# Head 1's input projections as seven block products instead of eight, with the sums of inputs formed beside the latent projections

## The chip, the cores and the metric

One Trainium2 chip, one core of it. The metric is the device time of one execution in microseconds (us), lower is better. The kernel computes one inference step of a one-layer encoder for 544 tokens (512 of a new stream, 32 of a running one).

The engines are named as in the profile: PE is the matrix engine (TensorE), DVE the VectorE, ACT the ScalarE, POOL the GpSimd; SP only issues transfers. Each engine takes its own row of instructions in order and waits at an instruction until what it needs is there.

## The reference, cut to what matters

```python
def token_mixer(x, s0, lat_past, kr_past, blk, lb, w_in, ...):
    proj = x @ w_in                       # x: 544 tokens x 2048 features
    hq, hf, hi, hg, cq, ckv, kr = jnp.split(proj, SPLITS, axis=-1)
    f = lb + (1.0 - lb) * jax.nn.sigmoid(hf)
    o_h, s_new = hgrn2_recurrence(heads(hq), heads(1.0 - f), heads(jnp.log(f)), heads(hi), s0, blk)
    o_h = rms_norm(o_h, ...) * jax.nn.silu(hg)
    ...                                   # latent attention from cq, ckv, kr -> o_a
    out = jnp.concatenate([o_h, o_a], axis=-1) @ w_out

def encoder(x, ...):
    h = layer_norm(x, ...)
    mix = token_mixer(h, ...)
    h = layer_norm(ALPHA * h + mix, ...)
    ff = conv_ffn(h, ...)                 # two projections up to 5632 features, one down
    h = layer_norm(ALPHA * h + ff, ...)
```

There are 8 recurrent heads and 8 attention heads. The change touches the projections `x @ w_in` of recurrent head 1 (its q, f, i and g columns, 128 each).

## The kernel before, in words

All products are in split form for accuracy: each 32-bit operand is written as a high part (`wh`, `aH`, made by a copy on ACT) and a low part (`wl`, `aL`, made by a subtraction on DVE), and three matmuls are summed (high x high, high x low, low x high). A weight piece is loaded by SP into one of three `raw` buffers (`load_raw`, L123), and ACT and DVE split it (`split_w`, L128).

The order of the stages is that of the code: layer norm and the projection cq (until about 78 us); ckv (`ckv_proj`, 77.9 to 104.8) and kr (`kr_proj`); the two projections q and f of head 0 (`head_qf(0)`, four weight pieces of 48 matmuls, from 112.7); four pairs of attention heads (`proj_pair`, `attend`); i and g of head 0 (`head_ig(0)`, beside the last `attend`); head 1 (296 to about 372); heads 2 to 7 (until 696); then the output projection (until about 850) and the convolutional FFN, which the change does not touch.

`weave` (L191) mixes two sequences in program order: after so many steps of the filling one, one step of the chain, such as `ckv_norm` (L487) with its two rows `lx` of the normalised latent, or `kr_rope`. A few instructions of `ckv_norm` are PE's: sums over the features (L441) after the first 24 matmuls of `head_qf(0)`, and a spread over partitions (L450, L451) after 72.

Heads 2 to 7 are projected in a divided form (`divided`, L828): the 2 x 2 blocks of the input (features x tokens, 272 tokens each) and of the weights are combined as in Winograd's form of Strassen's product, so that seven block products of 24 matmuls do instead of eight. The seven are named "11", "s1", "s2", "s4", "s3", "12", "22"; "s1" to "s4" use sums of input blocks, which are formed once (`sums_of_inputs`, L724): with t0 and t1 the two token halves of a feature row, and t0b, t1b those of the row 1024 features on, the sums are t0 - t1, t1b - t1 and two that follow from them. Each is split into a high and a low part. s1, s2 and s4 stay in SBUF; s3 goes through DRAM and is then laid over the second halves of `aH` and `aL` (`place_s3`). The weights' sums are formed per group: DVE adds blocks (L780) and POOL issues accumulating transfers (L782, L795). In the same place (`low`, L791) POOL issues up to two further accumulating transfers, the `forms`, by which block sums of `w_out` are prepared in DRAM for the output stage, which is divided too.

Heads 0 and 1 are done plainly (`N_PLAIN = 4` groups of two projections: 192 matmuls each). While head 1 is done, the sums of inputs are formed from the rows `h0` of the normalised input, reloaded from DRAM; beside it run `levels(0)`, `levels(1)` and `finish(0)`, the recurrences of heads 0 and 1. In `levels`, Kp and Qp are formed on DVE, then PE and DVE alternate through seven levels.

From head 2 on the order on PE, DVE and ACT is that of the code (`tc.manual_schedule`), by slots: each product has two, and `beside_from` says in which slots a step of `levels` or `finish` is put.

The memory for the recurrences (`gp`) opens when that of attention (`mp`) closes. Its tiles wait for the last users of what lay there, such as the store of `attend`'s last difference (L669, L670).

Of the kernel before, what the change touches and what calls it, by code (L numbers as in the profile page):

```python
# [15 lines left out]
P = 128  # L16
# [39 lines left out]
N_PLAIN = 4  # L56
# [3 lines left out]
def tile_encoder_step(ctx, tc, xp, xs, w_in, w_in4, w_kr, w_q_b, w_kv_b, w_out, w_out4, w_up, w_gate, w_down, w_down2,  # L60
# [16 lines left out]
    d3_dr = [dram.tile([P, 2, NI], F32, name=f"d3d{k}", tag=f"d3d{k}") for k in range(HK // 2)]  # L77
    sm_dr = [dram.tile([P, 3, 4, NI], F32, name=f"sm{i}", tag=f"sm{i}") for i in range(2)]
# [321 lines left out]
    with tc.tile_pool(name="mp", bufs=1) as mp, tc.tile_pool(name="psa", bufs=4, space=PSUM) as psa:  # L400
        cos = mp.tile([P, T], F32, name="cos")
        sin = mp.tile([P, T], F32, name="sin")
# [7 lines left out]
        ropes = [[mp.tile([P, TP], R, name=f"qr{g}{j}", tag=f"qr{g}{j}") for j in range(2)] for g in range(2)]  # L410

# [58 lines left out]
        def cq_norm():  # L470
            rb, rb2 = yield from rms_rows(sq_sum(cqx), 512)
            for k in range(4):
# [4 lines left out]
                h, l = split_act(x, bufs=4, pool=mp, th="qaH", tl="qaL")  # L477
# [9 lines left out]
        def ckv_norm():  # L487
            rb, rb2 = yield from rms_rows(c["kvs"], 256)
            for k in range(2):
                x = c["kv"][k]  # L490
                lx = mp.tile([P, NK], F32, name="lx", tag="lx", bufs=1)
# [7 lines left out]
                h, l = split_act(lx, bufs=2, pool=mp, th="latH", tl="latL", n=NK)  # L499
# [37 lines left out]
        def proj_pair(pr):  # L537
# [46 lines left out]
            vt = mp.tile([P, 6, 2, P], F32, name="vt", tag="vt")  # L584
# [13 lines left out]
        def softmax(sc, nq, keys):  # L598
            mx = mp.tile([P, 1], F32, name="mx", tag="mx", bufs=4)
            rs = mp.tile([P, 1], F32, name="rsum", tag="rsum", bufs=4)  # L600
            p = mp.tile([P, 512], F32, name="p", tag="p", bufs=3)
# [7 lines left out]
        def attend(pr):  # L609
            qn, qr, kn, vt = pairs[pr]  # L610
            o = mp.tile([P, 2, T], F32, name="o", tag="o")
# [67 lines left out]
        weave([ckv_proj(), kr_proj()], [cq_norm()], 0.5, tick)  # L679
        weave([head_qf(0)], [ckv_norm(), kr_rope()], 0.5, tick)  # L680
        while len(forms) > 24:
            form_next()
        run(proj_pair(0))
        weave([proj_pair(1)], [attend(0)], 2.0)
        weave([proj_pair(2)], [attend(1)], 2.0)
        weave([proj_pair(3)], [attend(2)], 2.0)
        weave([head_ig(0)], [attend(3)], 2.0)
# [12 lines left out]
    s3_dr = [dram.tile([P, 2, NI], F32, name=f"s3d{k}", tag=f"s3d{k}") for k in range(HK)]  # L700


    with tc.tile_pool(name="gp", bufs=1) as gp, tc.tile_pool(name="psg", bufs=1, space=PSUM) as psg:
# [9 lines left out]
        sums = {n: [gp.tile([P, 2, 4, NI], R, name=f"{n}{i}", tag=f"{n}{i}") for i in range(2)] for n in ("s1", "s2", "s4")}  # L713

        def part(n, k, i):
            return sums[n][k // 4][:, i, k % 4]

        def load_sums():
            for k in range(HK):
                for dst, kg, j in (("s1", k, 1), ("s2", k, 0), ("s4", HK + k, 0)):  # L720
                    dma(part(dst, k, 1).bitcast(F32), h0_dr[kg][:, H_[j]])
                dma(part("s1", k, 0).bitcast(F32), h0_dr[HK + k][:, H_[1]])

        def sums_of_inputs():  # L724

            load_sums()
            for k in range(HK):
# [304 lines left out]
        def early_form():  # L1032
            ticks[0] += 1
            if ticks[0] in (6, 9, 12, 15):
                form_next()
# [1621 lines left out]
```

## Time and profile before

| What | Before |
|---|---|
| Device time, median of 3 runs | 2337.82 us (2337.44 to 2337.97) |
| Profiled execution, its own time | 2336.92 us |
| Its span, first to last instruction | 2335.1 us |
| Mean granted PE clock | 0.994 |
| PE busy | 2295.9 us (98%) |
| DVE busy | 1713.1 us (73%) |
| ACT busy | 1095.4 us (47%) |
| POOL busy | 271.3 us (12%) |
| Moved by DMA | 474.57 MB, mean 203 GB/s |

The span is what the profile's times count from; the time of an execution holds a little more at both ends. A row of the profile names a line of the kernel, an engine, an operation, what it writes and what it reads; in brackets stands how long the engine was idle before it and what ended that. "Granted clock" is the share of full speed that the throttle gave PE. A DMA's time to landing runs from its issue to the arrival of its last byte.

### The profile page before, as it was taken

To read this page: it belongs to the slowest core of one execution; us is meant where nothing else is said; L and a number is where in the kernel's file an instruction comes from. 1 tells how busy PE (TensorE), PEld (TensorE's weight loads), DVE (VectorE), ACT (ScalarE), POOL (GpSimd) and SP (SyncE) were. 2 spreads that over 40 slices of the span, in tenths; PEclk is the share of its full clock that TensorE was granted. 3 is DMA by queue.
4 is the path that set the end of the run, shared out by engine and by line. 5 is a ranking of instruction groups with operands and counts; after the bars stand their busy time and mean duration, and the time that the engine had idled before them with its cause. 6 is when DMAs were issued, how large, how long until landed. Compare 5 with 4: busy or idle time off the path is not lost.

```text
span 2335.1 us, 44650 instructions
## 1 busy us (share of the span) xinstructions
PE 2295.9 (98%) x18258; PEld 2279.5 (98%) x18258; DVE 1713.1 (73%) x2393; ACT 1095.4 (47%) x1686; POOL 271.3 (12%) x335
## 2 busy tenths in 40 slices
PE   7999999999999999999999999999999999999997
PEld 7999999999999999999999999999999999999997
DVE  7455567777776878987777777777777677777776
ACT  6345434343444537655555555555555433333324
POOL 1011001111101111010000000100001111111102
PEclk9999999999999999999999999999999999999998
DMA  7432277676766756777667676776777999889832
GB/s 262 144 108 95 73 220 181 175 169 194 166 186 221 251 160 219 211 198 217 194 180 230 169 205 204 177 230 179 188 221 187 367 325 309 264 273 309 285 106 79
DMA packets 175773, 474.57 MB, mean 203 GB/s; under 512 B 16080, under 2 KB 80336, under 8 KB 168144
## 3 DMA queue, kind: packets, MB, share of 16 engines
q1 hardware_dynamic: 140368, 320.76, 39.7%
q0 software_dynamic: 35200, 150.94, 28.1%
q8 instruction: 144, 2.36, 0.4%
q14 instruction: 61, 0.50, 0.1%
HBM read 394.36 MB, written 91.34 MB: 208 GB/s over the span
## 4 chain that ended last, share of the span: by engine, by line
PE 92%; DVE 2%; ACT 2%; DMA 1%; issue 1%; POOL 0%; SPq 0%; ACTq 0%; DVEq 0%; POOLq 0%
PE main L1319 22%; PE acc L1319 17%; PE main L1350 11%; PE main L851 10%; PE main L146 10%; PE acc L1350 7%; PE acc L146 3%; PE s L916 2%; PE sb L1804 1%; PE main L1804 1%; PE main L591 1%; PE at L652 1%; PE at L621 1%; DMA xr<-wf1s 1%; PE main L578 0%
## 5 line engine op out<-in xcount | busy, mean ns | idle before, releaser
L1261 DVE TENSOR_TENSOR wl<-raw,wh 128x1024 fp32r<-128x1024 f32 x371 | 456.2, 1230 | 193.2 <-ACT wh L1260 192.9
L1260 ACT ACTIVATE wh<-raw 128x1024 fp32r<-128x1024 f32 x371 | 392.1, 1059 | 408.9 <-PE main L1319 99.3
L1319 PE MATMUL main<-op,wh 128*128 128x272 f32 x1408 | 265.4, 288 | 0.0
L1319 PE MATMUL acc<-ops,wh 128*128 128x272 f32 x1344 | 254.1, 288 | 0.0
L1319 PE MATMUL main<-ops,wh 128*128 128x272 f32 x1344 | 254.1, 288 | 0.0
L1319 PEld LDWEIGHTS main<-op,wh 128*128 128x128 f32 x1408 | 221.2, 188 | 0.0
L1319 PEld LDWEIGHTS acc<-ops,wh 128*128 128x128 f32 x1344 | 211.2, 188 | 0.0
L1319 PEld LDWEIGHTS main<-ops,wh 128*128 128x128 f32 x1344 | 211.1, 188 | 0.0
L1319 PE MATMUL main<-op,wl 128*128 128x272 f32 x704 | 203.1, 288 | 0.3 <-DVE wl L1261 0.3
L1319 PE MATMUL main<-ops,wl 128*128 128x272 f32 x672 | 193.9, 289 | 0.0
L1319 PE MATMUL acc<-ops,wl 128*128 128x272 f32 x672 | 193.9, 288 | 0.0
L1319 PE MATMUL acc<-op,wh 128*128 128x272 f32 x832 | 157.5, 288 | 1.0 <-ACT ea L1645 1.0
L1260 ACT ACTIVATE wh<-rawl 128x1024 fp32r<-128x1024 f32 x93 | 98.8, 1063 | 117.3 <-PE acc L1319 45.8
L146 PE MATMUL main<-aH,wh 128*128 128x272 f32 (+2 forms) x608 | 149.3, 297 | 0.3 <-ACT wh L316 0.2
L146 PE MATMUL main<-aH,wl 128*128 128x272 f32 (+2 forms) x608 | 147.8, 293 | 1.8 <-DVE wl L317 1.8
L146 PE MATMUL main<-aL,wh 128*128 128x272 f32 (+2 forms) x608 | 146.4, 292 | 1.0 <-DVE aL L305 1.0
L1261 DVE TENSOR_TENSOR wl<-rawl,wh 128x1024 fp32r<-128x1024 f32 x93 | 113.8, 1224 | 27.0 <-ACT wh L1260 26.9
L1319 PEld LDWEIGHTS main<-op,wl 128*128 128x128 f32 x704 | 132.4, 188 | 0.5 <-DVE wl L1261 0.5
L1319 PEld LDWEIGHTS acc<-op,wh 128*128 128x128 f32 x832 | 130.5, 188 | 1.2 <-ACT ea L1645 1.2
L793 DVE TENSOR_TENSOR wl<-raw,wh 128x1024 fp32r<-128x1024 f32 x84 | 103.1, 1227 | 35.9 <-ACT wh L788 35.0
L1319 PEld LDWEIGHTS main<-ops,wl 128*128 128x128 f32 x672 | 126.4, 188 | 0.0
L1319 PEld LDWEIGHTS acc<-ops,wl 128*128 128x128 f32 x672 | 126.4, 188 | 0.0
(513 smaller groups left out, 6090.8 us busy)
## 6 DMA issues: line engine op xcount, KB each, us to landing
raw<-in_w_in SPq DMA_DIRECT2D x76, 512.0 KB, 5.1
raw<-in_w_up SPq DMA_DIRECT2D x71, 512.0 KB, 5.2
raw<-in_w_gate SPq DMA_DIRECT2D x71, 512.0 KB, 4.8
raw<-in_w_down SPq DMA_DIRECT2D x67, 512.0 KB, 9.2
opd<-ohl SPq DMA_DIRECT2D x20, 1088.0 KB, 5.5
ops<-opd POOLq DMA_DIRECT2D x20, 1088.0 KB, 12.0
raw<-in_w_up POOLq DMA_DIRECT2D x35, 512.0 KB, 5.2
opd<-ohl SPq DMA_DIRECT2D x20, 816.0 KB, 6.4
```

Source lines behind the costliest of these rows:

```text
L146: PE.matmul(ps, ww[:, wcols[0]:wcols[1]], aa[:, hs[j]], start=first and i == 0, stop=last and i == 2, skip_group_check=True)
L591: PE.matmul(ps[:, j * 512:j * 512 + 256], l[k][:, a:b], r4(w[:, k:k + 1, :])[:, 0, :, 128:256], start=k == 0 and i == 0, stop=k == 1 and i ...
L621: PE.matmul(sc[:, :nk], qn[j][:, q0:q0 + P], kn[j][:, :nk], start=True, stop=False)
L652: PE.matmul(po[:, :P], vt[:, k, j, :], t[:, k * P:(k + 1) * P], start=k == 0, stop=k == b)
L793: V.tensor_tensor(out=wl, in0=self.t(self.key), in1=wh.bitcast(F32), op=ALU.subtract)
L851: PE.matmul(out, ww[:, k * P:(k + 1) * P], aa, start=name in ("11", "s1", "12") and k == 0 and q == 0, stop=k == HK - 1 and q == 2, skip_g ...
L916: PE.matmul(ps[:, j * 64:(j + 1) * 64], Kp[:, a:b], Qv[:, j * bt:(j + 1) * bt, 1, :], start=True, stop=True)
L1260: A.activation(wh, src, AF.Copy)
L1261: V.tensor_tensor(out=wl, in0=src, in1=wh.bitcast(F32), op=ALU.subtract)
L1319: PE.matmul(ps, ww[:, k * P:(k + 1) * P], aa, start=self.first and k == 0 and i == 0, stop=k == n - 1 and i == 2, skip_group_check=True)
L1350: PE.matmul(banks[:, 512 * u:512 * u + NI], ww[:, (u * n + k) * P:(u * n + k + 1) * P], aa, start=self.first and k == 0 and i == 0, stop=k ...
L1804: PE.matmul(self.bank, ww[:, k * P:(k + 1) * P], aa, start=self.first and k == 0 and i == 0, stop=k == HK - 1 and i == 2, skip_group_check ...
```

## The change

`N_PLAIN` goes from 4 to 2: head 1's two groups are divided too, so that 14 groups of seven products follow head 0. For this the sums of inputs must be there before head 1 begins.

- `sums_of_inputs` moves to the latent projections. `beside` takes a step of it after every second step of `ckv_proj`, `kr_proj` and `head_qf(0)`; each step handles a block row k of 8 in half: loads of two rows `h0`, four half-width sums on DVE; then two splits of full width and four stores to DRAM (`si_dr`). It works in tiles of attention that are not yet in use (`p`, `kn`, `o`, `vt`, `qr0`, `qr1`).
- The sums are loaded back: s1 and s2 under `head_ig(0)` and `attend(3)`, into a part of SBUF on the right side that the latent's tiles have left (`mpr`, then `smr`); s4 into `gp`; s3 is laid over `aH` and `aL` as before, from `si_dr`.
- `levels(0)` and `finish(0)` become steps in the slots of the divided part: `levels(0)` at slots 0 to 12, `finish(0)` and `levels(1)` both from slot 15.
- The four early `forms` under `head_ig(1)` are gone; the forms are issued two per group from head 1's first group on.
- In the output stage, the product "s2" of column group 2 moves ahead of "s4" of group 1, and two hooks come one item later.

```diff
-N_PLAIN = 4
+N_PLAIN = 2
...
+        def sums_of_inputs():
+            for k in range(HK):
+                tag, n, bufs = (("p", T, 3), ("kn", NK, 2))[k % 2]
+                a, b = (mp.tile([P, n], F32, name=tag, tag=tag, bufs=bufs)[:, :T] for _ in range(2))
+                dma(a, h0_dr[k])
+                dma(b, h0_dr[HK + k])
+                t0, t1, t0b, t1b = (x[:, h] for x in (a, b) for h in H_)
+                yield
+                minus(t1b, t1b, t1)
+                minus(t1, t0, t1)
+                opposite(t0, t1b, t0)
+                opposite(t0b, t0, t0b)
+                for x, names, (tag, n) in ((a, ("s2", "s3"), (("o", 2 * T), ("qr0", 2 * T))[k % 2]),
+                                           (b, ("s4", "s1"), (("vt", 12 * P), ("qr1", 2 * T))[k % 2])):
+                    hl = mp.tile([P, n], R, name=tag, tag=tag)[:, :2 * T].rearrange("p (i w c) -> p i w c", i=2, w=2)
+                    x2 = x.rearrange("p (w c) -> p w c", w=2)
+                    A.activation(hl[:, 0], x2, AF.Copy)
+                    V.tensor_tensor(out=hl[:, 1], in0=x2, in1=hl[:, 0].bitcast(F32), op=ALU.subtract)
+                    for w, name in enumerate(names):
+                        dma(si_dr[name][k // 4][:, :, k % 4], hl[:, :, w].bitcast(F32))
+                yield
...
-        weave([ckv_proj(), kr_proj()], [cq_norm()], 0.5, tick)
-        weave([head_qf(0)], [ckv_norm(), kr_rope()], 0.5, tick)
+        of_inputs = sums_of_inputs()
+        weave([beside(ckv_proj(), of_inputs, 2), beside(kr_proj(), of_inputs, 2)], [cq_norm()], 0.5, tick)
+        weave([beside(head_qf(0), of_inputs, 2)], [ckv_norm(), kr_rope()], 0.5, tick)
+        run(of_inputs)
...
+        mpr_stack.close()
...
+        for name in ("s1", "s2"):
+            load_sum(smr, name)
         weave([head_ig(0)], [attend(3)], 2.0)
...
-        of_inputs = sums_of_inputs()
-        weave([beside(head_qf(1), of_inputs, 2)], [levels(0)], 0.6)
...
-        weave([beside(head_ig(1), of_inputs, 2)], [levels(1), finish(0)], 1.2, early_form)
-        run(of_inputs)
-        place_s3()
         supply()
         for n in range(2):
             begin(n)
             complete(n)
+        load_sum(gp, "s4")
+        place_s3()
...
-            beside_from(0, finish(1), range(15))
-            for h in range(2, HEADS):
-                s0 = 28 * (h - 2) + 15
+            beside_from(0, levels(0), (0, 1, 3, 4, 6, 8, 9, 11, 12))
+            beside_from(15, finish(0), range(15))
+            for h in range(1, HEADS):
+                s0 = 28 * (h - 1) + 15
...
-            groups = [g for h in range(2, HEADS) for g in (divided_qf(h), divided_ig(h))]
+            groups = [g for h in range(1, HEADS) for g in (divided_qf(h), divided_ig(h))]
...
+        osteps += [(1, "12"), (1, "s1"), (1, "s2"), (2, "s2"), (1, "s4"), (1, "s3"), (1, "22")]
...
-                  3: [lambda: split_su("s2", 1)], 4: [lambda: split_su("s4", 0), lambda: split_su("s4", 1)],
-                  5: [lambda: split_21(range(4))], 6: [lambda: split_21(range(4, 8))],
+                  3: [lambda: split_su("s2", 1)], 4: [lambda: split_su("s4", 0)], 5: [lambda: split_su("s4", 1)],
+                  6: [lambda: split_21(range(4))], 7: [lambda: split_21(range(4, 8))],
```

The change moves instructions in the engines' rows. Before, SP's row where the weights of `head_qf(0)` are loaded: the third and fourth of its four pieces are the two loads of `raw` in one row, right behind the second and a form.

```order
L492 DMA lx<-in_latp 128x128
L125 DMA raw<-in_w_in 128x1024
L91 DMA wf3s_109<-in_w_out 16x8192
L125 DMA raw<-in_w_in 128x1024 x2
L91 DMA wf4s_113<-in_w_out 16x8192
L125 DMA raw<-in_w_q_b 128x768 x2
```

Now, SP's row behind the stores of block row 6 of the sums, up to the load of the third piece (`sis` are the sums in DRAM, `out_lat` the latent's output, `t<-t` the swapped halves of the rope).

```order
L494 DMA lx<-in_latp 128x128
L499 DMA out_lat<-lx 128x512
L500 DMA out_lat<-lx 128x32
L459 DMA t<-t 32x544
L460 DMA t<-t 32x544
L459 DMA t<-t 32x544
L460 DMA t<-t 32x544
L700 DMA sis_100<-qr_1628 256x1x272
L700 DMA sis_102<-qr_1628 256x1x272
L700 DMA sis_104<-qr_1633 256x1x272
L700 DMA sis_98<-qr_1633 256x1x272
L127 DMA raw<-in_w_in 128x1024
```

The load of the third piece stood ahead of the latent's stores and the rope's swaps; it now stands behind them and behind the stores of all eight block rows.

DVE's row before, at the splits of the third and fourth piece (the last `wl<-raw,wh 128x1024 x2`):

```order
L434 TENSOR_TENSOR t<-t 128x544
L135 TENSOR_TENSOR wl<-raw,wh 128x1024
L435 TENSOR_TENSOR t<-t 128x544
L135 TENSOR_TENSOR wl<-raw,wh 128x1024 x2
L444 TENSOR_SCALAR r_1371<-at 128x5
L523 TENSOR_TENSOR t<-t 128x544
```

And now, from block row 7 of the sums on:

```order
L186 SCALAR_TENSOR_TENSOR kn<-kn 128x272 x2
L495 SCALAR_TENSOR_TENSOR lx<-t,par,at 128x512
L497 SCALAR_TENSOR_TENSOR lx<-t,par,at 128x32
L698 TENSOR_TENSOR qr_1628<-kn,qr_1628 128x544
L698 TENSOR_TENSOR qr_1633<-kn,qr_1633 128x544
L215 TENSOR_TENSOR latL<-lx,latH 128x672
L465 TENSOR_TENSOR t<-t,sin 128x544
L467 TENSOR_TENSOR krs<-t 128x512
L467 TENSOR_TENSOR krs<-t 128x32
L532 TENSOR_TENSOR krl<-krs,krh 128x512
L137 TENSOR_TENSOR wl<-raw,wh 128x1024 x2
```

The two splits stood ahead of the first step of `ckv_norm` (L444); they now stand behind its last.

POOL's row before, where `attend(3)` ends (its difference is the second of the two `o<-o`) and the recurrences begin:

```order
L669 TENSOR_TENSOR o<-o 128x2x272 x2
L708 MEMSET attnT_3481 128x544
L708 MEMSET attnT_3482 128x544
L711 MEMSET kT 128x128
L91 DMA wf1s_99<-in_w_out 256x512
L91 DMA wf1s_101<-in_w_out 256x512
```

And now (`raw` are blocks of head 1's weights, `wf1s` the forms):

```order
L671 TENSOR_TENSOR o<-o 128x2x272
L796 DMA raw<-in_w_in 128x1024
L809 DMA raw<-in_w_in 128x1024
L93 DMA wf1s_107<-in_w_out 256x512
L93 DMA wf1s_109<-in_w_out 256x512
L671 TENSOR_TENSOR o<-o 128x2x272
L754 MEMSET attnT_3638 128x544
L754 MEMSET attnT_3639 128x544
L757 MEMSET kT 128x128
```

Four accumulating transfers now stand ahead of `attend(3)`'s difference on POOL, two for head 1's weights and two forms.

More of the change, by code (lines that the diff above doesn't have):

```diff
@@ L77, in tile_encoder_step @@
     d3_dr = [dram.tile([P, 2, NI], F32, name=f"d3d{k}", tag=f"d3d{k}") for k in range(HK // 2)]
+    si_dr = {n: [dram.tile([P, 2, 4, NI], F32, name=f"si{n}{i}", tag=f"si{n}{i}") for i in range(2)]
+             for n in ("s1", "s2", "s3", "s4")}
     sm_dr = [dram.tile([P, 3, 4, NI], F32, name=f"sm{i}", tag=f"sm{i}") for i in range(2)]
@@ L677, in tick, with beside @@
                 form_next()
-        weave([ckv_proj(), kr_proj()], [cq_norm()], 0.5, tick)
-        weave([head_qf(0)], [ckv_norm(), kr_rope()], 0.5, tick)
+        def sums_of_inputs():
[19 more added lines that the diff above has]
+                yield
+        def beside(main, side, every):
+            for n, _ in enumerate(main):
+                if n % every == every - 1:
+                    next(side, None)
+                yield
+        of_inputs = sums_of_inputs()
+        weave([beside(ckv_proj(), of_inputs, 2), beside(kr_proj(), of_inputs, 2)], [cq_norm()], 0.5, tick)
+        weave([beside(head_qf(0), of_inputs, 2)], [ckv_norm(), kr_rope()], 0.5, tick)
+        run(of_inputs)
         while len(forms) > 24:
             form_next()
+        ropes = [[t[:, j * T:j * T + TP] for j in range(2)]
+                 for t in (mp.tile([P, 2 * T], R, name=f"qr{g}", tag=f"qr{g}") for g in range(2))]
         run(proj_pair(0))
@@ L686, in tile_encoder_step, with load_sum @@
         weave([proj_pair(3)], [attend(2)], 2.0)
+        mpr_stack.close()
+        sr_stack = ExitStack()
+        smr = sr_stack.enter_context(tc.tile_pool(name="smr", bufs=1, side="right", reuse_waits="tile"))
+        sums = {}
+        def load_sum(p, name):
+            sums[name] = [p.tile([P, 8 * NI], R, name=f"{name}{i}", tag=f"{name}{i}").rearrange("p (i k c) -> p i k c", i=2, k=4)
+                          for i in range(2)]
+            for i in range(2):
+                dma(sums[name][i].bitcast(F32), si_dr[name][i])
+        for name in ("s1", "s2"):
+            load_sum(smr, name)
         weave([head_ig(0)], [attend(3)], 2.0)
@@ L1095, in tile_encoder_step @@
         out_first()
+    sr_stack.close()
     ph1.close()
```

67 lines of the change are left out of this document (15 added, 52 removed).

## The prediction

> **What bounds the kernel now.** I read the page first, then busy time by stage, then the chain of waits and the time lines of the engines around the two places that the change touches. The page says that TensorE (PE) is the bound: it is busy nearly all the time, and it is 92% of the chain that ended last.
>
> ```profile
> PE 2295.9 (98%) x18258; PEld 2279.5 (98%) x18258; DVE 1713.1 (73%) x2393; ACT 1095.4 (47%) x1686; POOL 271.3 (12%) x335
> PE 92%; DVE 2%; ACT 2%; DMA 1%; issue 1%; POOL 0%; SPq 0%; ACTq 0%; DVEq 0%; POOLq 0%
> ```
>
> So an edit pays by the matmuls it removes and costs by the stretches in which it leaves PE empty. Busy time by stage (columns: length, then busy time of each engine, granted clock, DMA share, GB/s) shows where PE has holes:
>
> ```profile
> 85.00:113.00 28.00, 28.00 (x227) 28.00 (x226) 13.02 (x20) 8.34 (x12) 0.74 (x1) 1.00 0.34 115
> 127.00:150.00 23.00, 23.00 (x181) 22.73 (x180) 8.49 (x14) 9.44 (x14) 1.75 (x2) 1.00 0.37 114
> 296.30:372.00 75.70, 72.45 (x575) 71.34 (x574) 58.55 (x141) 26.15 (x50) 8.41 (x10) 0.95 0.69 193
> 372.00:696.00 324.00, 322.90 (x2650) 321.23 (x2649) 233.68 (x402) 131.51 (x194) 43.84 (x50) 1.00 0.70 180
> ```
>
> The stage to which the sums of inputs move (85 to 150) has PE full and the other engines half empty; the stage they leave (296 to 372, head 1 done plainly) loses 3.25 us of PE and runs at a mean clock of 0.95. The chain through that stage:
>
> ```profile
> 296.51 1.36 POOL o L669
> 297.89 2.65 DMA d3d<-o
> 302.42 6.66 DMA s<-h0d
> 312.42 1.97 PE s L916 x8
> 314.73 3.13 PE main L146 x13
> 319.16 1.73 PE main L146 x13
> 320.88 0.84 PE s L916 x8
> 388.98 9.04 PE main L851 x72
> ```
>
> **Part 1, the eighth product.** Each of head 1's two groups takes 7 x 24 = 168 matmuls for 192: 48 fewer in all. 9.04/72 = 125.6 ns each: **-6.0**.
>
> **Part 2, the holes of the old stage.** PE's own rows, with the idle time before each in brackets:
>
> ```profile
> 312.42 1.97 PE L916 MATMUL s<-Qp,Kp 128*128 128x64 f32 x8 [3.19 <-DVE Kp L922]
> 375.52 0.74 PE L952 MATMUL sw<-ident,Kp 128*128 128x128 f32 x5 [0.75 <-DVE og L1009]
> 314.00:316.00 2.00, 2.00 (x10) 2.00 (x10) 1.23 (x4) 0.51 (x2) 0.00 (x0) 0.50 0.95 175
> 318.00:320.00 2.00, 2.00 (x17) 2.00 (x17) 0.81 (x3) 0.73 (x1) 0.88 (x1) 0.92 1.08 378
> ```
>
> The 3.19 us is a step of levels(0) behind sums that wait for h0 (the 6.66 us in the chain). It goes with the sums, and the 0.75 with the regrouping: **-3.9**. After it the clock stood at 0.50 until about 318: the same eight products took 1.97 and later 0.84, the same thirteen 3.13 and later 1.73, so half clock cost 1.1 + 1.4 and, with the smaller pieces between, about **3.1** us per such stall. Here I take it as gone, and charge it again for each new stall over 3 us.
>
> [...]
>
> **Part 3, a new wait at head_qf(0)'s third weight piece.** This decides the sign. PE, the two splitting engines and SP in this place before:
>
> ```profile
> 115.69 1.17 PE L441 MATMUL at<-ones,t 128*128 128x1 f32 x10
> 124.02 15.99 PE main L146 x127
> 109.99 1.23 DVE L135 TENSOR_TENSOR wl<-raw,wh 128x1024 fp32r<-128x1024 f32 x1 [1.31 <-ACT wh L134]
> 116.91 0.16 DVE L444 TENSOR_SCALAR r<-at 128x5 f32<-128x5 f32 x1 [1.20 <-PE at L441]
> 123.92 0.75 DVE L493 SCALAR_TENSOR_TENSOR lx<-t,par,at 128x512 f32<-128x512 f32 x1 [1.41 <-PE at L450]
> 310.52 0.44 DVE L184 SCALAR_TENSOR_TENSOR s_f<-s_f,s 128x272 f32<-128x272 f32 x1
> 107.97 0.72 DVE L435 TENSOR_TENSOR t<-t 128x544 f32<-128x544 f32 x1
> 296.23 1.06 ACT L134 ACTIVATE wh<-raw 128x1024 fp32r<-128x1024 f32 x1 [3.03 <-PE main L146]
> 95.70 5.54 SPq L125 DMA_DIRECT2D raw<-in_w_in  x2
> 118.35 0.58 SPq L458 DMA_DIRECT2D t<-t  x1
> raw<-in_w_in SPq DMA_DIRECT2D x76, 512.0 KB, 5.1
> hm<-in_hmask SPq DMA_DIRECT2D x1, 272.0 KB, 3.4
> cx<-catd SPq DMA_DIRECT2D x15, 272.0 KB, 5.3
> ```
>
> PE wants this piece 24 matmuls (3.0 us) after 124.02, at 127.0. Before, SP issued it at 95.70 and DVE had split it by 111.2: 16 us of cover. Now SP's order puts its load behind all the sums of inputs, and so behind the latent's chain. SP and DVE take their rows in order, so I walk them by the durations above. (a) DVE's row after L441's products (116.9) cannot move, since PE's order there has not. Behind it stand half of block row 5's sums (three passes of 0.36 from start to start, a copy on ACT, two of 0.72): done at about 120. (b) SP then has four writes, two swaps of the rope and four loads of h0 at 0.4 to 0.6 each, so row 6's inputs are asked for at 123.7 and land 3.4 to 5.3 later, at about 128. (c) DVE does row 6 (four half passes, copies, two of 0.72: 3.3), the second lx (0.75 and a little) and row 7: done at 133.5. (d) SP holds, ahead of the weights, row 6's writes, the second latent's load and stores, four swaps and row 7's four writes; the last twelve come after DVE's lx at about 132, at 0.4 to 0.6 each: the load goes out at about 138. (e) It lands 5.1 later, ACT's half takes 1.06: PE resumes at about 144.
>
> That is a stall of **17.0**. Lower bound 12: row 6's inputs in 3.4, issues of 0.33 where nothing waits, the weights in 3.4 too. Upper bound 22: each of three landings as crowded as the 6.66 in the chain. I take the middle because DMA had 0.37 of its engines busy here, and the change adds 16 loads and 32 stores of 272 KB, 13 MB. Half clock after it: **+3.1**. The fourth piece is then issued some 3 us behind the third, and PE needs it 6 us after: no further wait.
>
> The sums' other work (8 block rows of 3.1 us on DVE, 16 copies on ACT, those transfers) I cost at nothing: DVE was busy 13.02 of 28 and 8.49 of 23 there. If that cover went, DVE would be late by what does not fit, and it would show at the same pieces.
>
> **Part 4, a new wait at the head of divided head 1.** PE leaves head_ig(0) at about 296.3: the ACT row quoted above at 296.23 takes a weight buffer that PE's last piece of that head set free. Before, the plain head_qf(1) followed, with several pieces of PE's own work ahead of levels(0); now one product (24 matmuls, 3.0) stands there, and PE needs levels(0)'s Kp at 299.4.
>
> ```profile
> 287.97 1.23 DVE L135 TENSOR_TENSOR wl<-raw,wh 128x1024 fp32r<-128x1024 f32 x1 [2.05 <-ACT wh L134]
> 300.66 1.35 DVE L893 TENSOR_SCALAR Kp<-hproj 128x544 f32<-128x544 f32 x1 [0.68 <-DMA d3d<-o]
> 488.05 1.25 POOL L91 DMA_DIRECT2D wf1s<-in_w_out  x1
> 497.14 0.89 POOL L91 DMA_DIRECT2D wf2s<-in_w_out  x1 [7.85 <-issue]
> 514.35 1.26 POOL L91 DMA_DIRECT2D wf3s<-in_w_out  x1
> 526.15 0.88 POOL L91 DMA_DIRECT2D wf4s<-in_w_out  x1 [10.55 <-issue]
> ```
>
> Kp's space comes free when attend(3)'s difference (POOL, 1.36) has been stored (2.65): 300.6 before. In the new order POOL issues two accumulating transfers for w_out ahead of that difference. They are set free by a weight split that stands where the one at 287.97 stood. Of six such pairs in the trace the second transfer left POOL 9.1 us after the first at the soonest (488.05 to 497.14) and 11.8 at the latest (514.35 to 526.15). From a first one at 290 the difference runs at 300 to 302.7 rather than 296.5, space is free 4.0 later, at 304 to 306.7, and with Kp's 1.35 PE resumes at 305.4 to 308: 6 to 8.7 after 299.4. I take **+7.0**, and half clock **+3.1** (the one that part 2 took away). If POOL is not held, Kp comes at 302.0: 2.6.
>
> **Part 5, levels(1) and finish(0) in one group.** Elsewhere a group has one or the other. A group takes 324/12 = 27.0 us and 19.5 of DVE, of which 7 splits and 2 sums of 1.23 and 3 updates of 0.44 are 12.4; levels and finish of one head are then 2 x 7.1. Both at once make 26.6 of 27.0: DVE is full for one group, and late by whatever does not line up. Lower bound 0.75, what the same pair left PE idle before; upper bound 6, what two splits and two sums wait that find the queue full (4 x 1.23, and one of 0.72). I take **+2.5**, nearer the row.
>
> **Part 6, the output stage.** One step earlier and two block sums one slot later.
>
> ```profile
> 785.04 0.48 PE L1804 MATMUL main<-us,wh 128*128 128x272 f32 x2 [1.20 <-DVE za L1835]
> 791.92 0.36 PE L1804 MATMUL sb<-aH,wh 128*128 128x272 f32 x1 [0.62 <-ACT n_e L1164]
> ```
>
> These two waits should go (-1.8); two neighbours on one PSUM bank may bring one back, so **-0.9**, between -1.8 and +1.
>
> **The sum.** -6.0 - 3.9 - 3.1 + 17.0 + 3.1 + 7.0 + 3.1 + 2.5 - 0.9 = +18.8. The profiled execution took 2336.92, its span and what lies around it, 0.9 under the median of the runs shown, 2337.82. So 2355.7 against its own time, and **2356.6** as a median, slower by 0.8%. About 0.2% (4.7 us) is what a measurement of this kernel can tell from no change.
>
> **Rivals.**
> *The cover of part 3 holds* (other side): if SP gets the third piece's load out early enough for its halves to be ready, landed by about 125, part 3 costs nothing; and if POOL is not held, part 4 costs 2.6 with no half clock. Then -6.0 - 3.9 - 3.1 + 2.6 + 2.5 - 0.9 = -8.8: 2329.0. For it speaks that DVE and ACT are half idle here; against it, that the load stands in SP's order behind stores which wait for an lx that PE itself feeds at 124. It decides from a load issued before 120. Chance 0.07.
> *Part 3 holds its cover, part 4 does not*: -8.8 + 4.4 + 3.1 = -1.3, 2336.5, no difference that can be told. Chance 0.07.
> *Part 3 stalls, POOL is not held*: 2356.6 - 4.4 - 3.1 = 2349.1. For it: the first two accumulations have other neighbours here. Chance 0.14.
> *Crowded transfers*: with h0, stores and weights all in flight together, each landing is 6.66 and part 3 costs 22 or more, part 5 up to 6: 2356.6 + 5 + 3.5 = 2365.1. Chance 0.12.
>
> **How the numbers follow.** The forecast has 0.60. Slower by over 0.2% are it, the crowded case and the one without part 4: 0.86; the same 0.07; faster 0.07. The range leaves out the two cases of 0.07 below. From 2349.1, with part 3 some 4 short of its middle, it starts at 2345; it ends at 2367, the crowded case with part 4 at its upper bound.
>
> **What would show it.** In the profile after: PE's row at head_qf(0)'s 97th matmul with 12 to 22 us idle before it, released by ACT's wh of that piece, and a clock of 0.50 behind it; SP issuing that load at 135 or later; a second PE wait of 6 to 9 us at levels(0)'s first products, behind Kp, behind the stored difference; no 3 us wait in levels(0)'s second step. It is wrong if PE is full from 113 to 139 as before, or if the load of the third piece stands on SP before 120.

## The result and the profile after

| What | Before | After |
|---|---|---|
| Device time, median | 2337.89 us (2337.44 to 2339.33, 4 runs) | 2369.97 us (2369.49 to 2370.11, 4 runs) |
| Ratio after to before | | 1.0136 (95%: 1.0118 to 1.0153) |
| Span of the profiled execution | 2335.1 us | 2368.1 us |
| Mean granted PE clock | 0.994 | 0.987 |

The change costs 32 us, 1.4%. The forecast was 2356.6 with a range to 2367: the sign was right, and 13 us are missing. The page after, the engines:

```profile
PE 2297.0 (97%) x18210; PEld 2280.2 (96%) x18210; DVE 1725.8 (73%) x2393; ACT 1102.3 (47%) x1686; POOL 274.7 (12%) x339
```

The 48 matmuls are gone (18258 to 18210), but PE is busy no less (2297.0 for 2295.9): what was saved came back as half clock, and the mean granted clock is 0.987 for 0.994. Of PE's own rows that waited, these bear on the account (idle time before the row and its releaser in brackets):

```profile
146.54 0.82 PE L148 MATMUL main<-aH,wh 128*128 128x272 f32 x2 [19.39 <-ACT wh L136]
172.59 0.58 PE L580 MATMUL main<-latH,wh 128*128 128x336 f32 x2 [0.82 <-ACT kn L584]
328.83 1.41 PE L913 MATMUL sw<-hproj,Kp 128*128 128x128 f32 x5 [7.18 <-DVE Kp L907]
368.02 1.30 PE L913 MATMUL sw<-hproj,Kp 128*128 128x128 f32 x10 [0.79 <-ACT vT L971]
375.95 1.10 PE L930 MATMUL s<-Qp,Kp 128*128 128x64 f32 x8 [1.31 <-DVE S L983]
398.47 0.65 PE L928 MATMUL s<-Qp,Kp 128*64 128x64 f32 x8 [0.77 <-DVE tot L942]
705.01 1.27 PE L913 MATMUL sw<-hproj,Kp 128*128 128x128 f32 x10 [0.17 <-DVE Kp L907]
768.43 2.72 PE L1127 MATMUL sb<-ones,n_e 128*128 128x1 f32 x12 [6.26 <-DVE n_e L1138]
827.55 0.37 PE L1804 MATMUL sb<-aH,wh 128*128 128x272 f32 x1 [1.34 <-ACT n_e L1164]
834.43 0.49 PE L1804 MATMUL main<-us,wh 128*128 128x272 f32 x2 [0.62 <-DVE za L1835]
```

The first and third are parts 3 and 4 where the prediction put them. The 6.26 at 768 is in no part of it. Rows that both traces have divide the span: the row of the latent's product (172.59) stood at 150.83 (L578), the one at 705.01 at 681.65 (L899). So the latent stage cost 21.8, heads 1 to 7 another 1.6 (23.4 in all), the output stage and the rest 9.6 (33.0 at the end).

**Part 3 in the trace.** The chain of waits after, from the first step of `ckv_norm` to the third weight piece:

```profile
116.94 0.17 DVE r L446
123.98 4.70 DMA p<-h0d
134.38 2.52 DMA lx<-in_latp
138.65 0.57 SPq L700
141.28 4.12 DMA raw<-in_w_in
```

This is the walk (a) to (e): a sum behind L446, row 6's inputs asked for just ahead of 123.98 (forecast 123.7) and there at 128.7 (128), row 7, the second latent, the last four stores, the load at 141.28 (138), PE at 146.54 (144). What came later than forecast is the end of SP's row. The stores of row 6 begin at 131.69, and from there to the load of the third piece SP issued 15 transfers with hardly a gap, 0.64 each:

```profile
131.69 1.23 SPq L700 DMA_DIRECT2D sis<-o  x2
```

The landings in the chain were not longer than forecast: 4.70 where 3.4 to 5.3 were given, and 4.12 for the 5.1 of the weights. The DMA engines as a whole were busy at 0.93, though, where before it was 0.40; the window of the wait after, then the one of before (length, busy times, clock, DMA share, GB/s):

```profile
100.00:146.00 46.00, 27.15 (x219) 26.93 (x217) 27.32 (x51) 12.79 (x20) 3.18 (x2) 0.83 0.93 302
```

```profile
100.00:150.00 50.00, 50.00 (x399) 49.73 (x397) 20.57 (x31) 16.54 (x24) 5.06 (x4) 1.00 0.40 125
```

**Part 4 in the trace.** POOL's rows, and the chain beside them:

```profile
312.23 1.29 POOL L93 DMA_DIRECT2D wf1s<-in_w_out  x1
321.69 0.89 POOL L93 DMA_DIRECT2D wf1s<-in_w_out  x1 [8.17 <-issue]
323.86 1.32 POOL L671 TENSOR_TENSOR o<-o 128x544 f32<-128x544 f32 x1 [1.28 <-DMA catd<-o]
```

```profile
315.81 7.88 DMA catd<-o
325.21 2.53 DMA d3d<-o
```

The second form left POOL 9.46 us after the first, as forecast, and had gone by 322.6. But the store of `o`, which the difference overwrites, landed only at 323.7, after 7.88 us, so POOL had two holds that ended almost together: the store's ended 1.28 later.

**The unforeseen wait.** POOL loads the residual `za` for the output's layer norm. The chain after, then POOL's row and one of SP:

```profile
760.11 7.26 DMA za<-h0d
768.43 2.72 PE sb L1127 x12
771.15 5.20 PE sb L148 x24
```

```profile
759.48 2.76 POOL L1505 DMA_DIRECT2D za<-h0d  x5 [11.10 <-PE main L148]
755.80 0.52 SPq L1034 DMA_DIRECT2D sm<-sm  x1
```

And of before, POOL's row and the same products in the chain:

```profile
724.75 2.78 POOL L1505 DMA_DIRECT2D za<-h0d  x5
```

```profile
738.85 1.23 PE sb L1127 x12
740.08 3.13 PE sb L146 x24
```

Before, the five loads went out 14 us ahead of L1127's products, with no wait; now they go 9 us ahead of them. In the built program `za` lies at the same bytes of each partition in both kernels. Before, sums of inputs lay there, last read by PE long before. Since s1 and s2 have moved to `smr`, and s4 to lower addresses of `gp`, the tiles of the last head's `finish(7)` lie there now (`sm`, `vT`, `S`, `og`). The last use of these is the store of `sm`, issued at 755.80 and landed 3.1 us later, at 758.9, which is when the last of POOL's waits ended. The stall costs 6.26, and the same 12 and 24 products behind it took 2.72 and 5.20 for 1.23 and 3.13: 9.8 in all.

### The profile page after: what moved, and what is told of

Its sections match the earlier page's. It is cut to its first block, busy times and chain, and to the rows that moved or that the text cites. A ratio compares the mean times of both kernels' runs of the same rounds, so it can differ in the third digit from the quotient of the medians.

```text
span 2368.1 us, 44628 instructions
## 1 busy us (share of the span) xinstructions
PE 2297.0 (97%) x18210; PEld 2280.2 (96%) x18210; DVE 1725.8 (73%) x2393; ACT 1102.3 (47%) x1686; POOL 274.7 (12%) x339
## 4 chain that ended last, share of the span: by engine, by line
PE 90%; DMA 3%; DVE 3%; ACT 2%; issue 1%; SPq 1%; POOL 0%; ACTq 0%; DVEq 0%; POOLq 0%
PE main L1319 22%; PE acc L1319 17%; PE main L865 12%; PE main L1350 10%; PE main L148 8%; PE acc L1350 7%; PE acc L148 3%; PE s L930 2%; PE main L1804 1%; PE sb L1804 1%; PE main L593 1%; PE at L654 1%; PE at L623 1%; DMA xr<-wf1s 1%; DMA raw<-in_w_in 1%
## 5 line engine op out<-in xcount | busy, mean ns | idle before, releaser
L1261 DVE TENSOR_TENSOR wl<-raw,wh 128x1024 fp32r<-128x1024 f32 x371 | 456.0, 1229 | 194.8 <-ACT wh L1260 194.6
L1260 ACT ACTIVATE wh<-raw 128x1024 fp32r<-128x1024 f32 x371 | 392.5, 1059 | 410.4 <-PE main L1319 100.8
L807 DVE TENSOR_TENSOR wl<-raw,wh 128x1024 fp32r<-128x1024 f32 x98 | 120.3, 1228 | 43.6 <-ACT wh L802 42.5
L148 PE MATMUL main<-aH,wh 128*128 128x272 f32 (+2 forms) x480 | 122.5, 298 | 19.6 <-ACT wh L136 19.4
L865 PE MATMUL main<-s,wh 128*128 128x272 f32 x672 | 133.7, 296 | 0.0
L865 PE MATMUL main<-aH,wh 128*128 128x272 f32 x448 | 133.2, 297 | 0.0
L802 ACT ACTIVATE wh<-raw 128x1024 fp32r<-128x1024 f32 x98 | 103.3, 1055 | 62.5 <-DVE raw L794 58.0
L865 PE MATMUL main<-aH,wl 128*128 128x272 f32 x448 | 129.6, 289 | 0.0
## 6 DMA issues: line engine op xcount, KB each, us to landing
ops<-opd POOLq DMA_DIRECT2D x20, 1088.0 KB, 11.8
```

The costliest lines, as they stand in the source:

```text
L148: PE.matmul(ps, ww[:, wcols[0]:wcols[1]], aa[:, hs[j]], start=first and i == 0, stop=last and i == 2, skip_group_check=True)
L802: A.activation(wh, self.t(self.key), AF.Copy)
L807: V.tensor_tensor(out=wl, in0=self.t(self.key), in1=wh.bitcast(F32), op=ALU.subtract)
L865: PE.matmul(out, ww[:, k * P:(k + 1) * P], aa, start=name in ("11", "s1", "12") and k == 0 and q == 0, stop=k == HK - 1 and q == 2, skip_g ...
L1260: A.activation(wh, src, AF.Copy)
L1261: V.tensor_tensor(out=wl, in0=src, in1=wh.bitcast(F32), op=ALU.subtract)
```

## The experiments

Each is the changed kernel with the edit shown. Medians stand against 2369.97; the kernel before had 2336.8 to 2337.7 beside them.

**1. s4 in a buffer of its own** (the unforeseen wait)

```diff
-        load_sum(gp, "s4")
+        s4_stack = ExitStack()
+        sp4 = s4_stack.enter_context(tc.tile_pool(name="sp4", bufs=1, side="right", reuse_waits="tile"))
+        load_sum(sp4, "s4")
...
+    s4_stack.close()
```

> One change to the changed kernel: s4 lies in a pool of its own on the right side, below s1 and s2, so that the tile za of the output stage lies over s4, as before, and no longer over the tiles of the last head's finish. Theory (za waited for those tiles): the wait of 6.26 us before the first layer-norm sums of the output stage goes, and the half clock behind it (the 12 sums took 2.72 for 1.23, the 24 products after them 5.20 for 3.13): -9.5, about 2360.5 us. Rival (the new order of the output steps, or the forms that are issued later, make that stage late): the wait stays, 2370, within 1 us.

2361.04 us (2360.37 to 2361.32), ratio 1.0099 (1.0082 to 1.0116). POOL's first load of `za`, and PE's row that had waited 6.26 (no bracket: no wait):

```profile
717.85 0.57 POOL L1508 DMA_DIRECT2D za<-h0d  x1 [13.41 <-PE main L865]
```

```profile
762.30 1.39 PE L1130 MATMUL sb<-ones,n_e 128*128 128x1 f32 x12
```

The loads go out 41.6 us earlier, the wait is gone, and 8.9 us with it. The wait was where s4 lay, and nothing in the order of the output's steps.

**2. No forms in the divided head 1's first group** (part 4)

```diff
-                    for _ in range(2):
+                    for _ in range(2 if self.c > N_PLAIN else 0):
                         form_next()
```

> One change to the changed kernel: head 1's first divided group issues no forms; they come with the groups after it. Theory (the two accumulating transfers hold POOL, and crowd the store of attend(3)'s output on which its difference waits): the difference runs at about 318.5 and not 323.9, the wait of 7.18 us before the first products of levels(0) shrinks to about 2, and no half clock follows: -8, about 2362 us. Rival (the store is slow for other reasons, the loads of s3 into aH and aL and the first weights): the difference still waits until about 323, the gain is under 1.5 us, 2368.5 to 2370.

2361.04 us (2359.62 to 2363.92), ratio 1.0102 (1.0086 to 1.0117); the profiled span is 2362.1, 6.0 shorter. POOL's row, the store in the chain, PE's row and a window behind it:

```profile
318.87 1.37 POOL L671 TENSOR_TENSOR o<-o 128x544 f32<-128x544 f32 x1 [6.12 <-DMA catd<-o]
```

```profile
316.02 2.68 DMA catd<-o
```

```profile
323.86 1.27 PE L913 MATMUL sw<-hproj,Kp 128*128 128x128 f32 x10 [2.00 <-DVE Kp L907]
```

```profile
326.00:328.00 2.00, 2.00 (x11) 2.00 (x11) 1.40 (x4) 0.00 (x0) 0.00 (x0) 0.50 0.92 346
```

Without the forms the difference runs 5.0 us earlier, and the store of `o` takes 2.68 instead of 7.88: the forms had held POOL and had crowded the store as well. They are 5.2 of the 7.18. The rest stays, and behind 2.00 us of waiting the clock still halves.

**3. head_qf(0)'s weights loaded ahead of the sums' last rows** (part 3): the first three in `kr_proj`, the fourth at the first split

```diff
+        def split_ahead(kk):
+            w = split_w(raws_qf[kk], 4, 256)
+            if kk == 0:
+                raws_qf.append(load_raw(in_group(3, 0), 4, 256))
+            return w
-        yield from gemm(tiles, in_pieces(2 * h), act, ALLK)
+        yield from gemm(tiles, split_ahead, act, ALLK)
...
+                raws_qf.extend(load_raw(in_group(i, 0), 4, 256) for i in ((0,), (1, 2))[kk])
```

> One change to the changed kernel: the loads of the four weight pieces of head 0's first group are written ahead of the steps of the sums that come with the kr projection, so that they stand earlier in SP's row; all loads and stores of the sums stay where they are. Theory (SP's order, not the traffic, makes the third piece late): the wait of 19.39 us and its half clock of 2.4 go. Late next is the first weight piece of the first attention pair, whose load still stands behind the sums: 5 to 9 us and half clock there. In sum -10 to -15, 2355 to 2360 us. Rival (the transfers themselves are crowded): the third piece is issued early and still lands late, a wait of over 10 us stays there, and the sum is within 5 us of 2370.

2369.58 us, ratio 1.0136 (1.0121 to 1.0151): nothing.

```profile
157.49 0.82 PE L148 MATMUL main<-qaH,wh 128*128 128x272 f32 x2 [17.39 <-ACT wh L136]
151.11 1.06 SPq L127 DMA_DIRECT2D raw<-in_w_q_b  x2
```

The 19.39 is gone from `head_qf(0)`, and 17.39 stand at the next weights that SP loads, those of `proj_pair(0)`: issued at 151.11, behind the same last stores. My expectation named that piece, at 5 to 9 us; it is nearly as late as the third piece was.

**4 and 5. The 32 stores issued by ACT, or by POOL** (part 3: SP's row)

```diff
-                        dma(si_dr[name][k // 4][:, :, k % 4], hl[:, :, w].bitcast(F32))
+                        A.dma_start(si_dr[name][k // 4][:, :, k % 4], hl[:, :, w].bitcast(F32))
```

In the second of the two, `G.dma_start` stands for `A.dma_start`.

> One change to the changed kernel: the 32 stores of the sums are issued by ACT and not by SP; work, traffic and places in the program are the same. Theory (SP's order): with 32 fewer issues on SP, each 0.6 us and some of them waits, the weights' loads come early; the wait of 19.39 us and its half clock go, -22, about 2348 us; ACT issues between its copies and has room. Second theory (ACT gets late by the stores, which wait for DVE): waits of 1 to 8 us before head 0's first pieces, 2350 to 2358. Rival (the transfers are crowded): a wait of over 10 us stays, 2365 to 2370.

> One change to the changed kernel: the 32 stores of the sums are issued by POOL and not by SP or ACT. Theory (SP's row is the bottleneck of this stage): the weights of head 0's first group and of the first attention pair come early, the wait of 19.39 us goes, and none of over 5 us takes its place: 2349 to 2355 us. Second theory (the transfers are also at their limit, about 340 GB/s from 100 to 120 us): the sums end no earlier, and waits of 8 to 15 us in all stay between 113 and 160, wherever they fall: 2358 to 2365. A risk of its own: the latent's norm has one step on POOL behind the stores, and PE waits for it inside head 0's group.

2363.44 us, ratio 1.011 (1.0095 to 1.0125), and 2364.78, 1.0115 (1.01 to 1.013). With ACT, 12.2 us of waits in seven pieces from 113 to 144, six of them behind weight splits; with POOL, 11.6 in two:

```profile
123.52 0.82 PE L148 MATMUL main<-aH,wh 128*128 128x272 f32 x2 [5.64 <-ACT t L520]
138.29 2.07 PE L452 MATMUL at<-ident,r 128*128 128x128 f32 x8 [5.95 <-POOL r L447]
```

Off SP's row, the stores hold whatever else their new engine has to do: ACT its splits, POOL the small `r` of the latent's norm. The third piece's load now goes out at 99.77 and 100.70, ahead of the sums' last rows, and the 19.39 at that piece is gone; counted over the stage, 7 to 8 us of waiting are.

**6. The stores in pairs: 16 issues fewer, the same bytes**

```diff
-                    for w, name in enumerate(names):
-                        dma(si_dr[name][k // 4][:, :, k % 4], hl[:, :, w].bitcast(F32))
+                    dma(si_two[names[0] + names[1]][k // 4][:, :, :, k % 4], hl.bitcast(F32))
```

> The changed kernel, but the two sums of one step leave by one store of twice the size: 16 store issues on SP's queue fewer, the same bytes. If the number of SP's issues is what makes head_qf(0)'s weights late (0.6 us each: 16 x 0.6 = 9.6 us earlier), the 19.39 us wait falls to about 10 and the time to 2358-2362. If the traffic of the stretch from 100 to 145 us is what makes them late, the waits before 165 us keep their sum within 3 us and the time stays at 2367-2372.

2369.13 us, ratio 1.0134 (1.012 to 1.0148); the wait is 19.58.

```profile
140.24 1.03 SPq L127 DMA_DIRECT2D raw<-in_w_in  x1
```

The number of issues is worth nothing here: an issue that follows such double stores takes about 1 us or more in most places, where it took 0.6, and the load goes out only 1.0 us sooner (141.28 before).

**7. Those forms that are plain copies moved under attention**

```diff
-        weave([beside(head_qf(0), of_inputs, 2)], [ckv_norm(), kr_rope()], 0.5, tick)
+        weave([beside(head_qf(0), of_inputs, 2)], [ckv_norm(), kr_rope()], 0.5)
...
-        weave([proj_pair(1)], [attend(0)], 2.0)
+        weave([proj_pair(1)], [attend(0)], 2.0, tick)
```

> The changed kernel, but the copies of weights that the forms make are moved from the latent projections to the attention behind them: the same work, some 6 MB read and written and 6 issues on SP's queue less in the stretch from 100 to 165 us. If the traffic sets the wait (12 MB at 0.34 MB per us are up to 35 us of transfer), the 19.39 us wait goes almost wholly and the time falls to 2348-2354. If the number of SP's issues sets it, 6 x 0.6 = 3.6 us are gained, the wait is near 15.5 and the time 2365-2367.

2363.4 us, ratio 1.0112 (1.0098 to 1.0125).

```profile
147.72 0.82 PE L148 MATMUL main<-aH,wh 128*128 128x272 f32 x2 [13.54 <-ACT wh L136]
```

```profile
107.39 0.45 SPq L127 DMA_DIRECT2D raw<-in_w_in  x1
142.63 0.58 SPq L127 DMA_DIRECT2D raw<-in_w_in  x1
```

The third piece's load has moved in SP's row: it goes out at 107.39, in time, and PE works through that piece. The 13.54 stand at the fourth, whose load goes out at 142.63, behind the last stores; PE resumes no sooner than before (147.72 for 146.54). So the wait is shorter by about the 6 us of work of one piece, and no price of a byte follows from it. Ahead of the third piece had stood not 12 MB of copies, as I had reckoned, but four of 512 KB.

**8. Transfers added that nobody waits for**

```diff
+                for w in range(2):
+                    dma(spare[2 * k + w], h0_dr[HK * w + k])
```

> The changed kernel with 16 further copies of 272 KB from DRAM to DRAM (4.46 MB), one pair beside each step's two loads, which nothing waits for: the work is as before, only transfers and 16 issues are added. Pairing the stores showed that 16 issues are worth nothing. If the transfers of the stretch decide when head_qf(0)'s third weight piece lands, the wait of 19.39 us grows by 6 to 13 us (4.46 MB at about 0.34 MB per us is 13 us; 6 if half of it falls into gaps) and the time goes to 2376-2384. If SP's waits for the sums decide it, by DVE's order, the wait grows by less than 3 us and the time stays below 2373.

2365.69 us, ratio 1.0124 (1.011 to 1.0137): faster, if anything. The copies were issued from 48.9 to 78.1, ahead of the crowded stretch, so it does not tell what more bytes there would do. But the order of SP's row behind them shifted, and that tells something else:

```profile
109.63 0.91 SPq L127 DMA_DIRECT2D raw<-in_w_in  x2
```

The third and fourth pieces now go out at 109.63, and the 19.39 is gone. Left in the latent stage are 1.89, 8.71 and 2.27 at other places.

**9. Each paired store made twice: 8.9 MB more**

```diff
-                    dma(si_two[names[0] + names[1]][k // 4][:, :, :, k % 4], hl.bitcast(F32))
+                    for two in (si_two, si_again):
+                        dma(two[names[0] + names[1]][k // 4][:, :, :, k % 4], hl.bitcast(F32))
```

> The run with paired stores, and each paired store made a second time, to other buffers that nobody reads: 32 store issues on SP's queue in the same places as in the changed kernel, twice their bytes (8.9 MB more). The run with 16 further copies did not tell what it was made for: the copies were issued from 49 to 78 us, ahead of the crowded stretch, and the order on SP's queue changed with them. If the transfers of the stretch decide when the third weight piece lands, the wait of 19.58 us grows by 15 to 26 us (8.9 MB at about 0.34 MB per us is 26 us) and the time goes to 2383-2396. If SP's waits for the sums, by the order on its queue and on DVE's, decide it, the wait grows by less than 6 us and the time stays below 2376.

2394.13 us, ratio 1.0238 (1.022 to 1.0256).

```profile
171.99 0.82 PE L149 MATMUL main<-aH,wh 128*128 128x272 f32 x2 [44.84 <-ACT wh L137]
```

```profile
100.00:171.00 71.00, 27.14 (x218) 26.86 (x216) 29.70 (x53) 12.11 (x20) 2.92 (x2) 0.73 0.95 314
```

```profile
149.57 1.45 SPq L701 DMA_DIRECT2D sas4s<-vt  x1
164.58 1.36 SPq L128 DMA_DIRECT2D raw<-in_w_in  x1
```

The wait is 25.3 us longer than in run 6, and the load goes out 24.3 later, with the DMA engines busy at 0.95. Bytes do count: as many stores as in the changed kernel, each of twice the size, take up to 1.45 on SP where they took 0.6, and SP's row is longer by that. But the places are not the same. The loads for rows 3 and 7 of the sums stand behind the stores of rows 2 and 6 here (108.02 and 151.07), in run 6 ahead of them (100.31 and 124.68), so that these rows wait for one another. The 2.8 us per MB that come out (25.3 for 8.9) are bytes and order together; how much is bytes alone stays open.

**10 to 12. Causes removed together.** All stores on POOL and the copies later (run 5 with run 7); with runs 1 and 2 besides; and with `finish(0)` from slot 13 for part 5:

```diff
-            beside_from(15, finish(0), range(15))
+            beside_from(13, finish(0), range(15))
```

> As the kernel with the stores on POOL, and the plain copies of the forms (512 KB read and 512 KB written each), which ran beside the sums, now run under attention. Second theory (the transfers are at their limit): six copies fewer are 6 MB or some 18 us of full transfer less between 85 and 145, and the waits that the stores on POOL left shrink by most of their size, -5 to -10 against that kernel. Theory (SP's row alone): no more than 2 us against it.

> All in one: stores on POOL, forms later, no forms in the first divided group, s4 on the right side. If the causes are separate they add up: from the kernel with stores on POOL and forms later another -9.5 and -9, so about 2334 if that one is near 2352, 2341 if it is near 2359. If they are not separate (the forms that are put off crowd a later place, say the output stage, where one is read), less than 12 of the 18 us come.

> As the kernel before, with the first step of finish(0) two slots earlier (slot 13), so that its 15 steps meet those of levels(1) in other places. Theory (the waits of 0.79, 1.31 and 0.77 us in that group come from steps that meet on the one tile sw and on a full DVE): one or two of them go, -1 to -2.5 us. Rival (DVE is full there whatever the order): within 0.7 us.

2359.94 us (ratio 1.0094, 1.0079 to 1.0109), 2344.79 (1.0031, 1.0022 to 1.004) and 2343.42 (1.0021, 1.0011 to 1.0031). Runs 1 and 2 gave 15.2 together, of the 17.9 that they gave one by one. The waits of part 5 fell from 2.86 to 1.49. Left in the latent stage: 2.31 at L148 and 4.88 behind POOL's `r`.

**13 to 16. The same, with the stores of rows 4 and 5 back on SP,** so that POOL's `r` is free of them; with paired stores; again; and with the output stage's order as before:

```diff
-                        G.dma_start(si_dr[name][k // 4][:, :, k % 4], hl[:, :, w].bitcast(F32))
+                        (dma if k in (4, 5) else G.dma_start)(si_dr[name][k // 4][:, :, k % 4], hl[:, :, w].bitcast(F32))
```

> The copies moved as in the run before it, the stores of the sums issued by POOL except for the steps 4 and 5 (whose stores stood ahead of the small ckv sums on POOL), with s4 in a buffer of its own, no forms in the divided head's first group and finish(0) from slot 13 on. The run with all stores on POOL had 2343.4 with waits of 4.88 us on POOL's r and 2.31 on ACT's t. If these are all that is left, they fall to about 2 in sum, and the half clock behind them goes: 2335-2339, level with the kernel before. If SP's stores of steps 4 and 5 hold the weights again, a wait of 4 to 8 us on wh takes their place and the time is 2342-2347.

> As the run before it, with the two sums of one step in one store. If the number of issues still matters with the forms gone from the stretch, it is 1 to 4 us faster than the run before it (2332-2337); if only the bytes matter, it is the same within 1 us.

> The same kernel as kq_b_d_c, whose gain (ratio 0.9985, interval 0.9976 to 0.9994) is below what I called measurable. If the gain is real, the ratio comes out at 0.998 to 0.9995 again; if not, at or above 1.

> kq_b_d_c, and the order of the output projection's steps and of its splits put back as in the kernel before. The prediction took the new order to be what would end the two waits of 1.20 and 0.62 us in the output stage; they are there still (1.32 and 0.62 in kq_b_d_c). If the order has no part in them, the time is the same within 1 us; if the new order does shorten what would otherwise be a longer wait, it is 1 to 4 us slower, with a wait above 2 us between 775 and 805 us.

2334.19 us (ratio 0.9985, 0.9976 to 0.9994), 2343.46 (1.0026, 1.0016 to 1.0036), 2335.8 (0.9995, 0.9986 to 1.0004) and 2335.83 (1.0001, 0.9992 to 1.001). So the repaired kernel is level with the one before; the gain of the first of these was not confirmed. Paired stores made it slower by 9 us between the medians; its first wait is 6.81 where the run beside it had 3.77 in its profiled execution (2341.25, the slowest of its 11), and what made the rest of the difference stays open. The repaired kernel's rows (the second run):

```profile
118.59 0.82 PE L148 MATMUL main<-aH,wh 128*128 128x272 f32 x2 [1.83 <-ACT t L520]
148.22 0.52 PE L148 MATMUL main<-qaH,wh 128*128 128x272 f32 x2 [2.13 <-ACT hproj L387]
309.11 2.15 PE L913 MATMUL sw<-hproj,Kp 128*128 128x128 f32 x10 [2.11 <-DVE Kp L907]
793.74 0.37 PE L1807 MATMUL sb<-aH,wh 128*128 128x272 f32 x1 [0.65 <-ACT n_e L1167]
```

With the old order of the output's steps, the two waits there are 1.73 and 0.62, with the new one 0.65 and 0.62: the new order is worth a microsecond at most, which the times can't tell.

## Why the prediction was right and wrong

**Failed: part 6**, "These two waits should go (-1.8) ... so -0.9, between -1.8 and +1". The output stage cost 9.8 in one stall that I had not looked for. I had read the edit to the order there, and took the memory of the output stage as untouched because its code is. What the change moves is the place of s1, s2 and s4, and with it what `za` is laid over; run 1 took that alone away and gave 8.9 back. Nor did the two small waits go: after, they are 1.34 and 0.62 for 1.20 and 0.62. Of the 13 us that the forecast lacked, this term is 10.7 (9.8 + 0.9). By the rows, the rest is 1.7 in the latent stage and 2.0 in heads 1 to 7 (these are the profiled executions, 33.0 apart where the medians are 32.1).

**Mechanism right, size short: part 3.** Forecast 17.0 and 3.1 of half clock, 20.1; by the rows of the latent stage, 21.8. The wait is 19.39. The step that was too short is (d): the last twelve transfers were to start at 132 and take 0.5 each, so that the load would go out at 138. Ahead of them stood row 6's four stores, which SP could issue only from 131.69 to 134.27, and the second latent's load and the ten behind it took 0.63 each from 134.38 on: 141.28, so 3.3 late, of which the weights' landing gave 1.0 back. (In step (c) the terms as given add up to 135 and more, not to 133.5; DVE did finish at 135.69, but SP's row ended later still and decided.) The middle was chosen "because DMA had 0.37 of its engines busy", the share of before; the change fills the stretch to 0.93. Yet no landing in the chain was crowded, so this is not shown to be what was short.

What the runs show of the cause is the place in SP's row. Where the third piece's load left SP at 112.77 or sooner (runs 3, 4, 5, 7, 8), the 19 us at that piece are gone; where it left at 140.24 or later (the changed kernel, runs 6 and 9), they are there. In runs 3 and 7 a wait of 17.39 or 13.54 stands at the next weights behind the stores instead; in runs 4 and 5, where the stores do not stand in SP's row at all, 7 to 8 us of waiting go. The number of issues decides nothing here (run 6: 16 fewer, and the load 1.0 sooner), and what the bytes do by themselves is not separated from the order (run 9).

**Right in size, with a second way: part 4.** 7.18 for 7.0; by POOL's own hold alone it would have been 5.9, the last 1.28 is the store's, so that the figure comes out closer than the working deserves. The forms held POOL for 9.46, within the 9.1 to 11.8 of the old pairs, and the store of `o` that they crowded held it as long. Without them 2.00 remain (run 2), near the 2.6 forecast for a POOL that is not held.

**Right: parts 1, 2 and 5.** The matmuls are 48 fewer, the 3.19 and the 0.75 are gone; part 5's three waits are 2.87 for 2.5, and they fell to 1.49 with `finish(0)` two slots earlier (run 12).

**The half clock was priced too evenly**: 3.1 for each stall over 3 us. By the windows PE worked at half clock for about 4.5 us from 146.54, 10 from 328.83, 7 from 768.43, half of each lost. The excess at 328, 1.9, is most of why heads 1 to 7 came out at +1.6 and not at -0.4. And in run 2 it stays behind a wait of only 2.00.

The rivals in which part 3 or part 4 held are excluded by the waits themselves. The crowded case came nearest (2365.1) by luck: the landings of 6.66 that it rests on are not in the chain, and it lacks the term that failed too.

What is left of the saving shows in the repaired kernel (the second run) by the two rows that divide the span: they stand at 158.71 and 681.92 for 150.83 and 681.65 before. Heads 1 to 7 take 7.6 us less, and the latent stage 7.9 more: its waits, 1.83 and 2.13 the longest, and the half clock behind these two use the saving up.

## What to carry to other kernels

When a change moves tiles between memory pools, list what each later tile now lies over and when its last user ends, a store to DRAM included: a stage whose code is untouched can get a new wait (6.26 here). When work is added beside a stage, read the new order of each issuer's row: here the place of one load, behind stores that wait for another engine, made the largest wait (19.39), and neither the landing of the load (4.12) nor the number of issues (16 fewer left 19.58) did. Moving that load forward by itself only handed the wait to the next one behind the same stores (17.39 in run 3).

## What the runs showed of the hardware

In these runs the clock halved behind shorter waits than the 3 us that I had taken: 1.83, 2.13 and 2.11 in the repaired kernel, 1.84 in the same with the old order of the output's steps, 2.00 in run 2. The windows below show where it did and where it did not, first two of the repaired kernel around its 1.83, then one of the same kernel with the old order of the output's steps, right behind a wait of 2.33 (119.30). The last two are the changed kernel's behind the 7.18:

```profile
118.00:119.00 1.00, 0.41 (x2) 0.41 (x3) 1.00 (x3) 1.00 (x3) 0.00 (x0) 0.57 0.99 345
121.00:122.00 1.00, 1.00 (x8) 1.00 (x7) 0.45 (x2) 0.00 (x0) 0.46 (x1) 0.72 1.10 350
```

```profile
119.00:121.00 2.00, 1.70 (x13) 1.70 (x14) 1.27 (x2) 1.74 (x3) 0.00 (x0) 1.00 1.13 352
```

```profile
326.00:338.00 12.00, 9.17 (x42) 9.20 (x43) 5.12 (x8) 0.00 (x0) 1.48 (x3) 0.50 0.79 299
338.00:342.00 4.00, 4.00 (x33) 4.00 (x32) 2.06 (x5) 1.36 (x2) 0.00 (x0) 0.90 0.22 80
```

The stretches of half clock differ in length. In the repaired kernel the means 0.57 and 0.72 put the start of the first at 118.14 and its end at 121.56, 3.4 later. The next stretch, behind the 2.13, runs from 148.86 (0.93 in 148 to 149) to 152.28 (0.86 in 152 to 153), again 3.4. The one behind the 2.11 lasts 6.8 (309.3 to 316.1). In the changed kernel the three stretches, at the waits of 19.39, 7.18 and 6.26, are 20.5, 13.7 and 10.2 long, and each began while PE still waited.

So the length of a wait alone does not decide. The kernel with the old order kept its clock full behind the 2.33 (1.00 in 119 to 121), and halved it at 148.3 (0.66 in 148 to 149) at its shorter wait of 1.84, which ended at 147.93. Nor does it decide how long PE works at half clock behind it: 3.0 us behind the 1.83, 4.5 behind the 19.39, 9.9 behind the 7.18. What else has a part is not shown.

With SP as the issuer of all the sums' transfers, the DMA engines were busy at 0.93 in the changed kernel (302 GB/s, 100 to 146) and at 0.95 in run 9 (314 GB/s, 100 to 171). Fewer issues brought nothing (run 6: 2369.13 for 2369.97), while other issuers brought 6.5 and 5.2 us (runs 4 and 5): what they changed is which transfers stand ahead of the weights, whose third load went out at 99.77 and 100.70 for 141.28.
